# Two products by tiles, a pinned order of early casts, squares and copies, one pipeline for eight chunks

## The chip, the cores and the metric

The kernel runs on one core of one Trainium2 chip. The metric is the device time of one execution in microseconds (us); lower is better. A core has five engines that run independent instruction streams: TensorE (PE, matmuls; the load of its stationary operand is shown as PEld), VectorE (DVE), ScalarE (ACT), GpSimd (POOL), and a sync engine (SP) whose queue starts most of the transfers. Each stream is executed in the order in which it was written down; an instruction that waits holds up what stands behind it on its engine. Results of TensorE lie in eight banks of PSUM, all else in SBUF.

## What is computed

One layer on a sequence of 1024 tokens of width 1024, in float32: a feed-forward block, a mixer (a gated convolution on half of the channels, a gated delta rule with four heads on the other half), another feed-forward block, a norm. Cut to what matters:

```python
h = h + 0.5 * swiglu_ffn(rmsnorm(h, ffn1_norm), ffn1_w_in, ffn1_w_out)
u = rmsnorm(h, mix_norm) @ w_mix_in
cb, cc, ch, gq, gk, gv, gz, gb, ga = split(u)
y_conv = short_conv_mixer(cb, cc, ch, conv_short_w, conv_out_norm)      # 3 taps, norm over groups of 64
# q, k, v pass a causal convolution of 4 taps and silu; then, chunk by chunk,
# a triangular solve, products with a state that is carried on, norm, gate silu(z)
y_gdn = gated_deltanet_mixer(gq, gk, gv, gz, gb, ga, gdn_conv_w, ...)
h = h + concatenate([y_conv, y_gdn]) @ w_mix_out
h = h + 0.5 * swiglu_ffn(rmsnorm(h, ffn2_norm), ffn2_w_in, ffn2_w_out)
return rmsnorm(h, final_norm)
# swiglu_ffn(x): gate, up = split(x @ w_in);  (silu(gate) * up) @ w_out
```

## The kernel before

**Products.** Activations lie transposed, in tiles of 128 channels x 512 tokens; the tokens are two halves. Each float32 operand is split into a rounded high part (`hi`, `whi`, a cast on ScalarE) and a low part (`lo`, `wlo`, a subtraction on VectorE; `split`, lines 99 to 104), and one product of a tile is three matmuls of 128x512 (`mm3`, lines 190 to 194). Projections with two weight blocks and two token halves are done as 2x2 block products with seven multiplications instead of eight (`Pair`): products 1 and 2 take the first half of the tokens alone (`run_p1`, `run_p2`), 5 and 6 sums of halves with differences of weights (S1 with T1, nS2 with T2), 7 S3 with T3, 4 A22 with T4, 3 S4 with B22. T1 to T4 are made by GpSimd from raw weights in a ring of four buffers, then split; raw weights lie in a ring of eight, split ones in rings of seven. The first norm enters with `norm1` and `split1`; the second token half waits for its norm factor `rb`, which TensorE spreads over the partitions (L243), and then `sums` makes S1, nS2, S3, S4, A22 on VectorE and GpSimd (lines 293 to 320). `c22` at L389 is the first result of product 7.

**Order.** The program is written as lists of steps with a load, a preparation and a run (`task`, `run_tasks`); a scheduler then places the instructions on each engine by its own estimate of times. `tc.keep_in_program_order` pins an instruction behind those of its engine that were written before it. `later(n, f)` runs f after n further groups of three matmuls.

**Stages.** The first feed-forward block takes its first 100 us to start (`first_heads`, `by_tokens`: squares by tokens of the second half on ScalarE, L233; `begin2`: gains, L290). Then follow its body, its second product, the q, k, v projection (690 to 822 us) with the convolution of its first token half in `done`, and the delta rule: `build` makes the matrices of one chunk of 128 tokens, `solve` inverts, `finish` and `scan` carry the state through. The stage around 822 to 960 us builds chunks 0 to 3, then 4 and 5, with projections of z and of the short convolution (`rest`, through `pump`) between the steps at a rate `PACE`; `late` brings the convolution of the second token half. The scans of chunks 0 to 3 and of 4 to 7 are two pipelines (`inverse_and_scan`), the second beside the output projection `mix_out`. The second feed-forward block begins near 1250 us; the end of the kernel multiplies by the last factor, two quarters of the tokens after another, with one PSUM tile for both.

## Time and profile before

| | before |
|---|---|
| median of 3 executions | 1906.28 us (1905.80 to 1906.45) |
| the profiled execution, its span | 1906.43 us, 1904.4 us |
| TensorE busy in the span | 1816.6 us (95%) |
| VectorE, ScalarE, GpSimd busy | 1337.0 (70%), 747.3 (39%), 732.2 us (38%) |
| mean clock granted to TensorE | 0.981 of full speed |

A busy share is an average over stages with different limits, and TensorE's times overlap. So the views below go by stretches: which instruction waits there, and for which other.

### The profile page before, as it was taken

The numbers are of one execution on the slowest core, as the hardware profiler recorded it, in microseconds if no ns is written. First come the engines' busy times: TensorE is split into PE (matmuls) and PEld (weight loads), VectorE is DVE, ScalarE is ACT, GpSimd is POOL, SyncE is SP. The second block draws the span as 40 slices with busy tenths as digits, with TensorE's granted clock in tenths as the row PEclk, the third lists the DMA queues.
The fourth block names the chain that finished last, engine by engine and source line by source line (L and its number), as shares of the span: only waits on it lengthen the run. The fifth ranks groups of instructions, "written<-read, shape, count | busy, mean of one in ns | idle before, by whom it ended". The sixth has DMA issues, their size and how long they took to land.

```text
span 1904.4 us, 25000 instructions
## 1 busy us (share of the span) xinstructions
PE 1816.6 (95%) x8512; PEld 1483.8 (78%) x8512; DVE 1337.0 (70%) x1997; ACT 747.3 (39%) x1518; POOL 732.2 (38%) x514
## 2 busy tenths in 40 slices
PE   5799999999999998989899999999999999999997
PEld 4578888888888886777788888777788888888886
DVE  4876566657765888877868566787766666777666
ACT  5422232323434554367343333552222222344443
POOL 1464445445341434233321002035454455434243
PEclk9999999999999999999899989999999999999998
DMA  7143434345984543368744375422443434388642
GB/s 281 42 165 107 144 110 158 116 141 182 314 275 141 166 139 105 128 202 258 233 149 131 111 261 188 157 95 96 132 164 115 137 111 165 130 294 285 210 133 94
DMA packets 195663, 312.44 MB, mean 164 GB/s; under 512 B 27984, under 2 KB 50512, under 8 KB 195536
## 3 DMA queue, kind: packets, MB, share of 16 engines
q1 hardware_dynamic: 192080, 305.54, 48.4%
q10 hardware_dynamic: 3456, 5.31, 0.9%
q8 instruction: 67, 1.10, 0.2%
q14 instruction: 60, 0.49, 0.1%
HBM read 228.44 MB, written 82.33 MB: 163 GB/s over the span
## 4 chain that ended last, share of the span: by engine, by line
PE 44%; DVE 4%; issue 1%; DMA 1%; ACT 1%; POOL 1%; SPq 0%; POOLq 0%; DVEq 0%; ACTq 0%
PE ps_ps L191 10%; PE ps_ps L193 10%; PE ps_ps L192 10%; PE ps_mm L191 3%; PE ps_mm L193 3%; PE ps_mm L192 3%; DVE wlo L103 1%; PE ps_aux L879 1%; DVE lo L103 1%; PE ps_aux L921 0%; PE ps_aux L1147 0%; PE ps_mm L1199 0%; PE ps_aux L1146 0%; PE ps_mm L1185 0%; PE ps_aux L885 0%
## 5 line engine op out<-in xcount | busy, mean ns | idle before, releaser
L191 PE MATMUL ps_ps<-hi,whi 128*128 128x512 f32 x1400 | 551.2, 394 | 22.1 <-DVE c L389 12.3
L193 PE MATMUL ps_ps<-hi,wlo 128*128 128x512 f32 x1400 | 550.6, 394 | 12.6 <-DVE wlo L103 12.6
L192 PE MATMUL ps_ps<-lo,whi 128*128 128x512 f32 x1400 | 550.1, 393 | 4.8 <-DVE lo L103 4.7
L103 DVE TENSOR_TENSOR wlo<-T,whi 128x512 fp32r<-128x512 f32 x244 | 239.3, 994 | 145.3 <-ACT whi L102 144.0
L103 DVE TENSOR_TENSOR wlo<-raw,whi 128x512 fp32r<-128x512 f32 x280 | 261.6, 952 | 101.6 <-ACT whi L102 98.5
L191 PEld LDWEIGHTS ps_ps<-hi,whi 128*128 128x128 f32 x1400 | 265.6, 190 | 84.0 <-issue 10.2
L193 PEld LDWEIGHTS ps_ps<-hi,wlo 128*128 128x128 f32 x1400 | 265.9, 190 | 71.2 <-DVE wlo L103 15.6
L192 PEld LDWEIGHTS ps_ps<-lo,whi 128*128 128x128 f32 x1400 | 265.6, 190 | 62.2 <-DVE lo L103 7.2
L110 POOL TENSOR_TENSOR T<-raw 128x512 f32<-128x512 f32 x144 | 225.9, 1570 | 229.3 <-DMA raw<-w_out 87.5
L193 PE MATMUL ps_ps<-ghi,wlo 128*128 128x512 f32 x616 | 241.2, 392 | 0.8 <-DVE wlo L103 0.8
L191 PE MATMUL ps_ps<-ghi,whi 128*128 128x512 f32 x616 | 241.2, 392 | 0.0
L192 PE MATMUL ps_ps<-glo,whi 128*128 128x512 f32 x616 | 240.9, 391 | 0.0
L102 ACT CAST whi<-raw 128x512 fp32r<-128x512 f32 x280 | 169.3, 618 | 61.7 <-DMA raw<-w_out 17.2
L102 ACT CAST whi<-T 128x512 fp32r<-128x512 f32 x244 | 146.4, 617 | 78.4 <-POOL T L110 45.0
L191 PE MATMUL ps_mm<-hi,whi 128*128 128x512 f32 x384 | 160.3, 417 | 4.8 <-ACT whi L102 3.9
L103 DVE TENSOR_TENSOR glo<-raw,ghi 128x512 fp32r<-128x512 f32 x154 | 129.8, 844 | 46.7 <-ACT ghi L102 45.5
L193 PE MATMUL ps_mm<-hi,wlo 128*128 128x512 f32 x384 | 152.9, 399 | 0.8 <-DVE wlo L103 0.8
L192 PE MATMUL ps_mm<-lo,whi 128*128 128x512 f32 x384 | 152.9, 398 | 0.0
L193 PEld LDWEIGHTS ps_ps<-ghi,wlo 128*128 128x128 f32 x616 | 115.8, 188 | 27.6 <-DVE wlo L103 2.1
L192 PEld LDWEIGHTS ps_ps<-glo,whi 128*128 128x128 f32 x616 | 115.9, 188 | 25.5
L191 PEld LDWEIGHTS ps_ps<-ghi,whi 128*128 128x128 f32 x616 | 115.8, 188 | 25.3
L110 POOL TENSOR_TENSOR T<-raw,T 128x512 f32<-128x512 f32 x50 | 71.3, 1426 | 165.8 <-DMA raw<-w_in 135.2
(222 smaller groups left out, 2271.2 us busy)
## 6 DMA issues: line engine op xcount, KB each, us to landing
raw<-w_in SPq DMA_DIRECT2D x264, 256.0 KB, 4.5
raw<-w_out SPq DMA_DIRECT2D x154, 256.0 KB, 4.2
raw<-w_qkv SPq DMA_DIRECT2D x36, 256.0 KB, 3.3
f1S<-S SPq DMA_DIRECT2D x33, 256.0 KB, 4.9
raw<-f1A SPq DMA_DIRECT2D x33, 256.0 KB, 3.6
raw<-f1S SPq DMA_DIRECT2D x33, 256.0 KB, 3.5
f2S<-S SPq DMA_DIRECT2D x33, 256.0 KB, 4.9
raw<-f2A SPq DMA_DIRECT2D x33, 256.0 KB, 4.7
```

Source lines behind the costliest of these rows:

```text
L102: tc.keep_in_program_order(nc.scalar.copy(out=hi, in_=src))
L103: nc.vector.tensor_tensor(out=lo, in0=src, in1=hi.bitcast(F32), op=ALU.subtract)
L110: tc.keep_in_program_order(nc.gpsimd.tensor_tensor(out=out, in0=in0, in1=in1, op=op))
L191: nc.tensor.matmul(out=ps, lhsT=whi, rhs=xhi, start=start, stop=False, skip_group_check=True)
L192: nc.tensor.matmul(out=ps, lhsT=whi, rhs=xlo, start=False, stop=False, skip_group_check=True)
L193: nc.tensor.matmul(out=ps, lhsT=wlo, rhs=xhi, start=False, stop=stop, skip_group_check=True)
L879: nc.tensor.matmul(out=ps[:, sl], lhsT=lhs[:, sl], rhs=rhs[:, sl], start=start, stop=stop)
```

## The change

The squares by tokens, the gains of `begin2` and the copies of the first products of the first five pairs are pinned in the order written. Products 5 and 6 of the first two pairs of each block run by tiles: for each of four tiles k the product T1 with S1[k] and T2 with nS2[k] (`both`), with S1[k] split as soon as it exists. `sums(1)` and `sums(2)` become tasks at other places. The convolution of v for the first half of the tokens leaves `qkv_pair` and is done from a stored copy in `late_convs`; v's transfer into a chunk stands at a later step of `build`. The rate `PACE` falls, the reduce of `conv_norm` comes three groups later, all eight chunks go through one pipeline of scans, the split of the second block's first half runs inside the last output projection, and the last factor gets two PSUM tiles.

```diff
-PACE = (3.0, 2.6)
+PACE = (2.8, 2.2)
...
             for i, tile_ in enumerate(src):
-                nc.scalar.activation(out=tile_, in_=tile_, func=AF.Square, accum_out=tot[:, i:i + 1])
+                tc.keep_in_program_order(
+                    nc.scalar.activation(out=tile_, in_=tile_, func=AF.Square, accum_out=tot[:, i:i + 1]))
...
-            nc.scalar.activation(out=h2[k], in_=h2[k], func=AF.Copy, scale=self.gain(k))
+            tc.keep_in_program_order(
+                nc.scalar.activation(out=h2[k], in_=h2[k], func=AF.Copy, scale=self.gain(k)))
...
+                    b["S1"][k] = split(s1, slot)
                     b["nS2"][k] = split(s2, slot)
-                for k in range(KH):
-                    b["S1"][k] = split(h[1][k], slot)
...
-            nc.scalar.copy(out=self.p1[:, 3:HALF + 3], in_=self.x_ps)
+            ins = nc.scalar.copy(out=self.p1[:, 3:HALF + 3], in_=self.x_ps)
+            if self.pinned:
+                tc.keep_in_program_order(ins)
...
+        def both(self, k):
+
+            if k == 0:
+                self.z, self.y = psum(), psum()
+            ks = slice(k * P, (k + 1) * P)
+            for ps, t, s in ((self.z, "T1", "S1"), (self.y, "T2", "nS2")):
+                w = self.w[t]
+                mm3(ps, w[0][:, ks], w[1][:, ks], *self.x.b[s][k], k == 0, k == KH - 1)
+            if k == KH - 1:
+                self.w.pop("T1"), self.w.pop("T2")
+                self.u2 = temp4(F32, "u2")
+                nc.vector.tensor_tensor(out=self.u2[:, 3:HALF + 3], in0=self.y, in1=self.p1[:, 3:HALF + 3], op=ALU.add)
...
-            for n, two in enumerate(zip(*(p.body() for p in pairs[a:a + 2]))):
-                if a == 0 and n in (1, 2):
-                    task(None, lambda n=n: norm2.then(lambda: x.sums(n, norm2.rb)))
-                for t in two:
-                    task(*t)
+            products = list(zip(*(p.body() for p in pairs[a:a + 2])))
+            if a == 0:
+
+                for one, two in zip(*products[:2]):
+                    task(None, one[1], one[2])
+                    task(None, two[1])
+                for k in range(KH):
+                    task(lambda k=k: [p.both(k) for p in pairs[:2]])
+            for n, two in enumerate(products):
+                if a == 0 and n == 1:
+                    task(None, lambda: norm2.then(lambda: x.sums(1, norm2.rb)))
+                if a > 0 or n > 1:
+                    for t in two:
+                        task(*t)
+                if a == 0 and n == 2:
+                    task(None, lambda: norm2.then(lambda: x.sums(2, norm2.rb)))
...
+            for p in early:
+                p.pinned = True
...
+        v_dr = [dram.tile([P, HALF + 3], F32, name=f"v_dr{n}") for n in range(HEADS)]
...
-                    conv4(n + i, 0, t1, temp(F32, "cv"))
+                    if n < 2 * HEADS:
+                        conv4(n + i, 0, t1, temp(F32, "cv"))
+                    else:
+                        nc.sync.dma_start(out=v_dr[n + i - 2 * HEADS], in_=t1[:, 0:HALF + 3])
...
-            for g, dst in ((1, kT), (0, qT), (2, vT)):
+            for g, dst in ((1, kT), (0, qT)):
...
+            yield
             yield
...
+            nc.sync.dma_start(out=heads(vT), in_=qkv_dr[2][hf][:, :, ts])
             pq2 = flip(qT)
...
-            later(4, reduce)
+            later(7, reduce)
...
-            for n in (4, 5, 6, 7, 0, 1, 2, 3, 8, 9, 10, 11):
+            first = [(n, 0, v_dr[n - 8]) for n in (8, 9, 10, 11)]
+            for n, hf, src in first + [(n, 1, u_dr[n]) for n in (4, 5, 6, 7, 0, 1, 2, 3, 8, 9, 10, 11)]:
                 u = halo(F32, "u")
-                nc.sync.dma_start(out=u[:, 0:HALF + 3], in_=u_dr[n])
+                nc.sync.dma_start(out=u[:, 0:HALF + 3], in_=src)
                 yield
-                conv4(n, 1, u, mx.tile([P, HALF], F32, name="cv", tag="acc", bufs=3))
+                conv4(n, hf, u, mx.tile([P, HALF], F32, name="cv", tag="acc", bufs=3))
...
-                next(rest, None)
+                if next(rest, rest) is rest:
+                    tick()
...
         def inverse_and_scan(c):
+            if c == CPH:
+                for _ in side:
+                    pass
             yield from finish(c)
             yield from scan(c)
+            scanned.add(c)
...
-        drive(pipeline([build(c) for c in range(CPH)], 3), PACE[0], late, 1)
+        builds = pipeline([build(c) for c in range(CPH)], 3)
+        for _ in range(6):
+            next(builds)
+            pump(PACE[0])
+            next(late), next(late)
+        drive(builds, PACE[0], late, 1)
...
-        drive(pipeline([inverse_and_scan(c) for c in range(CPH)], 5), PACE[1], side, 1)
-        for _ in side:
-            pass
+        scans = pipeline([inverse_and_scan(c) for c in range(NCH)], 5)
+        while CPH - 1 not in scanned:
+            next(scans)
+            pump(PACE[1])
+            next(side, None)
...
-                task(lambda u=u: run(u, 1))
+                task(lambda u=u: run(u, 1), also and (lambda u=u: also(u)))
...
-        for n in range(4):
+        for n in range(6):
             tick()
             next(scans)
...
-        task(None, lambda: [x2.split1(d) for d in range(KT)])
-        mix_out(1, 1)
+        mix_out(1, 1, lambda u: [x2.split1(d) for d in (2 * u, 2 * u + 1)])
...
-        last[1].rb = psum()
...
+        rbs = [psum() for _ in range(2)]
         for i in range(2):
             for b in range(2 * i, 2 * i + 2):
-                nc.tensor.matmul(out=last[1].rb[:, b * P:(b + 1) * P], lhsT=rs[:, b:b + 1].broadcast_to([P, P]),
+                nc.tensor.matmul(out=rbs[i][:, b * P:(b + 1) * P], lhsT=rs[:, b:b + 1].broadcast_to([P, P]),
                                  rhs=ident, start=True, stop=True)
+            last[1].rb = rbs[i]
             scale_out(1, slice(2 * i * P, (2 * i + 2) * P))
```

The order of instructions on ScalarE at the start of the first block: `hi<-h` are the casts of the first half's tiles for product 2, `xtok` the squares by tokens, `p_...` the copies of first products. Before:

```order
L102 CAST whi<-raw 128x512 x2
L233 ACTIVATE xtok,tot<-xtok 128x512 x6
L351 COPY p_439<-ps_ps 128x512
L233 ACTIVATE xtok,tot<-xtok 128x512 x2
L102 CAST whi<-raw 128x512
L351 COPY p_441<-ps_ps 128x512
L351 COPY p_443<-ps_ps 128x512
L351 COPY p_445<-ps_ps 128x512
L290 ACTIVATE h<-h,vs 128x512 x2
L351 COPY p_466<-ps_ps 128x512
L102 CAST whi<-raw 128x512
L102 CAST hi<-h 128x512
```

and now:

```order
L102 CAST whi<-raw 128x512 x2
L102 CAST hi<-h 128x512 x4
L234 ACTIVATE xtok,tot<-xtok 128x512 x8
L102 CAST whi<-raw 128x512
L352 COPY p_443<-ps_ps 128x512
L352 COPY p_445<-ps_ps 128x512
L352 COPY p_447<-ps_ps 128x512
L352 COPY p_449<-ps_ps 128x512
L352 COPY p_470<-ps_ps 128x512
L102 CAST whi<-raw 128x512
```

Four casts stand ahead of all squares, and the squares ahead of all copies; before, the first of these casts was behind them.

VectorE at the start of the q, k, v projection: the last rows up to the first `c` of product 7 (`s` are the sums S4, `T_...` the weight differences, `u` the results of product 6). Before:

```order
L103 TENSOR_TENSOR lo<-h,hi 128x512 x4
L380 TENSOR_TENSOR u_6428<-ps_ps,p_6123 128x512
L103 TENSOR_TENSOR lo<-s_6297,hi 128x512
L103 TENSOR_TENSOR lo<-s_6305,hi 128x512
L103 TENSOR_TENSOR lo<-s_6313,hi 128x512
L103 TENSOR_TENSOR lo<-s_6321,hi 128x512
L103 TENSOR_TENSOR wlo<-T_6430,whi 128x512
L103 TENSOR_TENSOR wlo<-T_6436,whi 128x512
L103 TENSOR_TENSOR wlo<-T_6461,whi 128x512
L103 TENSOR_TENSOR wlo<-T_6486,whi 128x512
L103 TENSOR_TENSOR wlo<-raw,whi 128x512 x2
L389 TENSOR_TENSOR c_6508<-ps_ps,p_6089 128x512
```

and now:

```order
L103 TENSOR_TENSOR wlo<-T_6388,whi 128x512
L103 TENSOR_TENSOR wlo<-T_6406,whi 128x512
L103 TENSOR_TENSOR lo<-h,hi 128x512 x4
L103 TENSOR_TENSOR lo<-s_6341,hi 128x512
L378 TENSOR_TENSOR u_6462<-ps_ps,p_6093 128x512
L103 TENSOR_TENSOR lo<-s_6349,hi 128x512
L378 TENSOR_TENSOR u_6470<-ps_ps,p_6127 128x512
L103 TENSOR_TENSOR lo<-s_6357,hi 128x512
L103 TENSOR_TENSOR lo<-s_6365,hi 128x512
L103 TENSOR_TENSOR wlo<-T_6478,whi 128x512
L103 TENSOR_TENSOR wlo<-T_6490,whi 128x512
L405 TENSOR_TENSOR c_6508<-ps_ps,p_6093 128x512
```

The two `wlo<-raw` ahead of `c` are gone from there, and two differences T have moved ahead of the low parts `lo`.

The sync queue in the build stage (`qkv_dr20` is v after its convolution, `gd_...` the tiles of a chunk, loaded from q, k, v; `u` the inputs of the late convolution). Before:

```order
L937 DMA st_kg0_7346<-gd_7306 128x512
L937 DMA st_kd0_7349<-gd_7317 128x512
L937 DMA st_qg0_7347<-gd_7303 128x512
L944 DMA gd_7307<-qkv_dr10_292 128x4x128
L944 DMA gd_7304<-qkv_dr00_290 128x4x128
L937 DMA st_lt0_7351<-gd_7319 128x512
L790 DMA qkv_dr11_293<-cv_7464 128x512
L993 DMA diag_l0_7394<-dl_7481 128x4x32
L937 DMA st_at0_7350<-gd_7314 128x512
L944 DMA gd_7310<-qkv_dr20_294 128x4x128
```

and now:

```order
L820 DMA qkv_dr20_294<-cv_7470 128x512
L1265 DMA z_dr1_7240<-s_7548 128x512
L1312 DMA u_7551<-u_dr5_305 128x515
L970 DMA st_qg0_7327<-gd_7283 128x512
L977 DMA gd_7286<-qkv_dr10_292 128x4x128
L820 DMA qkv_dr20_294<-cv_7505 128x512
L1312 DMA u_7582<-u_dr6_306 128x515
L820 DMA qkv_dr11_293<-cv_7524 128x512
L1265 DMA z_dr0_7239<-s_7655 128x512
L1039 DMA gd_7289<-qkv_dr20_294 128x4x128
L1312 DMA u_7662<-u_dr7_307 128x515
```

Stores of v's convolution and loads of its inputs stand between a chunk's transfers now, and the load of v (`gd<-qkv_dr20`) behind the last of those stores.

## Rows read from the trace of the kernel before

**Rows 1.** Busy time by stretch, whole kernel; columns: stretch and its length, then busy time and instructions of PE, weight load, DVE, ACT, POOL, then the clock that TensorE was granted (1.00 is 2.4 GHz), the share of DMA engines busy and GB/s.

```profile
238.00:333.00 95.00, 95.00 (x421) 78.65 (x420) 62.58 (x70) 27.34 (x50) 49.28 (x32) 1.00 0.40 133
822.00:960.00 138.00, 124.44 (x602) 101.18 (x602) 107.53 (x240) 81.63 (x208) 53.24 (x44) 0.94 0.76 244
1092.00:1120.00 28.00, 25.30 (x194) 21.80 (x195) 12.34 (x28) 9.51 (x26) 3.27 (x2) 0.76 0.54 160
1250.00:1300.00 50.00, 43.27 (x178) 34.03 (x177) 46.01 (x56) 24.18 (x43) 24.75 (x15) 0.93 0.18 59
```

**Rows 2.** Timeline, TensorE between 38 and 46 us: start, length, line, operation, count, and in brackets the idle time ahead of it and what ended that.

```profile
38.03 0.96 PE L191 MATMUL ps_ps<-hi,whi 128*128 128x512 f32 x3 [1.86 <-ACT hi L102]
40.90 0.80 PE L192 MATMUL ps_ps<-lo,whi 128*128 128x512 f32 x1 [1.92 <-DVE lo L103]
41.50 0.63 PE L193 MATMUL ps_ps<-hi,wlo 128*128 128x512 f32 x1
...
45.76 0.62 PE L191 MATMUL ps_ps<-hi,whi 128*128 128x512 f32 x1
```

**Rows 3.** Timeline, ScalarE in the same stretch: a copy of a first product, which had waited for TensorE, and the first of the late casts.

```profile
31.45 0.58 ACT L351 COPY p<-ps_ps 128x512 f32<-128x512 f32 x1 [3.83 <-PE ps_ps L193]
...
37.33 0.65 ACT L102 CAST hi<-h 128x512 fp32r<-128x512 f32 x1
```

**Rows 4.** Timeline, VectorE (first four rows) and GpSimd (last two) in the first feed-forward block, from the first sum with the second norm factor to the first c of product 7.

```profile
52.12 0.69 DVE L300 TENSOR_TENSOR h<-h,ps_ps 128x512 f32<-128x512 f32 x1 [0.95 <-PE ps_ps L243]
...
57.65 1.19 DVE L103 TENSOR_TENSOR lo<-h,hi 128x512 fp32r<-128x512 f32 x1
...
63.37 0.68 DVE L103 TENSOR_TENSOR lo<-h,hi 128x512 fp32r<-128x512 f32 x1
...
87.82 0.68 DVE L389 TENSOR_TENSOR c<-ps_ps,p 128x512 f32<-128x512 f32 x1
...
56.61 3.38 POOL L110 TENSOR_TENSOR s<-h 128x512 f32<-128x512 f32 x2 [1.23 <-DVE h L301]
...
72.19 3.90 POOL L110 TENSOR_TENSOR T<-raw 128x512 f32<-128x512 f32 x2 [9.90 <-DVE wlo L103]
```

**Rows 5.** Waits of TensorE between 46 and 100 us: line that waited, what ended the wait, total, number, longest.

```profile
PE ps_ps L193 <- DVE wlo L103: 7.0, 2, 6.1
PE ps_ps L191 <- DVE c L389: 2.9, 1, 2.9
```

**Rows 6.** Timeline, VectorE at the start of the q, k, v projection, the same places.

```profile
693.28 1.27 DVE L300 TENSOR_TENSOR h<-h,ps_ps 128x512 f32<-128x512 f32 x2
...
736.31 0.68 DVE L389 TENSOR_TENSOR c<-ps_ps,p 128x512 f32<-128x512 f32 x1
```

**Rows 7.** Waits of TensorE at the start of that projection (690 to 745 us).

```profile
PE ps_ps L193 <- DVE wlo L103: 3.0, 2, 2.2
PE ps_ps L191 <- DVE c L389: 2.5, 1, 2.5
```

**Rows 8.** Start of the second feed-forward block: the waits of TensorE for low parts of weights (1255 to 1300 us), and the timeline row of TensorE behind its wait for c.

```profile
PE ps_ps L193 <- DVE wlo L103: 2.6, 2, 2.2
...
1297.06 0.47 PE L191 MATMUL ps_ps<-hi,whi 128*128 128x512 f32 x1 [2.94 <-DVE c L389]
```

**Rows 9.** Costliest groups of instructions between 790 and 825 us, shapes apart: the filter taps and the first scaling of the convolution there (busy time, mean of one).

```profile
L787 DVE SCALAR_TENSOR_TENSOR cv<-u,vs,cv 128x512 f32<-128x512 f32 x12 | 9.0, 749 | 1.1 <-ACT cv L785 0.9
...
L785 ACT ACTIVATE cv<-u,vs 128x512 f32<-128x512 f32 x4 | 2.9, 722 | 0.0
```

**Rows 10.** The longest wait of TensorE between 790 and 825 us.

```profile
PE ps_ps L191 <- DVE c L389: 1.9, 1, 1.9
```

**Rows 11.** Waits of TensorE in the build stage (822 to 960 us), the two longest.

```profile
PE ps_mm L1185 <- ACT sq L1180: 4.5, 1, 4.5
PE ps_aux L885 <- DMA gd<-qkv_dr: 3.1, 1, 3.1
```

**Rows 12.** Timeline of the sync queue in the build stage: a store of the convolution (L790), and behind it the load of one chunk's k and q (L944).

```profile
903.84 0.32 SPq L790 DMA_DIRECT2D qkv_dr<-cv  x1
904.25 1.23 SPq L944 DMA_DIRECT2D gd<-qkv_dr  x2
```

**Rows 13.** Waits of TensorE from 1200 to 1245 us, where the attention output is projected for the second half of the tokens.

```profile
PE ps_mm L191 <- ACT whi L102: 3.0, 1, 3.0
...
PE ps_mm L193 <- DVE wlo L103: 0.8, 1, 0.8
```

**Rows 14.** Timeline, VectorE in that stretch: low parts of the normalised first half (lo<-h) ahead of those of the projection's own operands (lo<-raw, wlo<-raw).

```profile
1206.35 1.89 DVE L103 TENSOR_TENSOR lo<-h,hi 128x512 fp32r<-128x512 f32 x3
...
1212.99 2.49 DVE L103 TENSOR_TENSOR lo<-raw,hi 128x512 fp32r<-128x512 f32 x4
```

**Rows 15.** Timeline, the end of the kernel, all engines.

```profile
1892.96 1.22 PE L1461 MATMUL ps_ps<-cs,last_rs 128*128 128x128 f32 x4 [0.18 <-POOL last_rs L1458]
...
1894.62 2.05 DVE L1430 SCALAR_TENSOR_TENSOR h<-h,vs,ps_ps 128x256 f32<-128x256 f32 x5 [1.65 <-ACT rbs L1424]
1894.67 2.09 POOL L1428 TENSOR_TENSOR h<-h,rbs 128x256 f32<-128x256 f32 x3 [0.92 <-ACT rbs L1424]
...
1896.82 1.19 PE L1461 MATMUL ps_ps<-cs,last_rs 128*128 128x128 f32 x4 [2.63 <-POOL h L1428]
...
1898.45 2.05 DVE L1430 SCALAR_TENSOR_TENSOR h<-h,vs,ps_ps 128x256 f32<-128x256 f32 x5 [1.78 <-ACT rbs L1424]
```

More of the change, by code (lines that the diff above doesn't have):

```diff
@@ L328, in __init__ @@
             self.x, self.srcs, self.first, self.done = x, srcs, first, done
-            self.r, self.t, self.w = {}, {}, {}
+            self.r, self.t, self.w, self.pinned = {}, {}, {}, False
         def get(self, *names):
@@ L1302, in pipeline @@
                         yield
+        scanned = set()
         def inverse_and_scan(c):
+            if c == CPH:
+                for _ in side:
+                    pass
             yield from finish(c)
             yield from scan(c)
+            scanned.add(c)
         def drive(main, n_main, side, n_side):
@@ L1343, in tile_hybrid, with mix_out @@
         norms2 = [Norm(h2[0], "mm"), Norm(h2[1])]
-        def mix_out(part, hf, bank="mm"):
+        def mix_out(part, hf, also=None):
+            bank = "mm"
             ys, w = [], {}
@@ L1377, in mix_out @@
                 task(lambda u=u: run(u, 0), lambda u=u: ready(u), lambda u=u: loads(u))
-                task(lambda u=u: run(u, 1))
+                task(lambda u=u: run(u, 1), also and (lambda u=u: also(u)))
         run_tasks()
-        scans = pipeline([inverse_and_scan(c) for c in range(CPH, NCH)], 5)
-        for n in range(4):
+        for n in range(6):
             tick()
@@ L1390, in tile_hybrid @@
         mix_out(0, 1)
-        left = [len(tasks)]
         def between():
```

## The prediction

> **What bounds the kernel now.** I read the views in this order: busy shares and slices on the page, busy time by stretch, TensorE's waits in each stretch, and the timelines around the longest waits. In the middle of a feed-forward block TensorE is never idle at full clock: 421 instructions fill 95.00 us [rows 1], so 0.226 us is the pace of one 128x512 product instruction. The same number of matmuls stands in the changed program, so time can only come from waits, from the clock that falls in them, and from the two ends. The waits sit where a stage begins. The build stage (822 to 960 us) is 138.00 long with 124.44 busy at a clock of 0.94, the chain of scans at the join 28.00 with 25.30 at 0.76, the start of the second block 50.00 with 43.27 at 0.93 [rows 1]. A mean clock of 0.94 with levels of 1.2 and 2.4 GHz says that 12% of the stretch ran at the lower level, 16.6 us, of which half, 8.3, is lost; with 13.6 idle the build stage gives at most 21.9. The join likewise: 13.4 us at the lower level, 6.7 lost, 2.7 idle, at most 9.4.
>
> **The change part by part.**
>
> *Early casts, squares and copies.* TensorE stops for 1.86 us on a cast (hi, ScalarE) and 1.92 on the low part (lo, VectorE), and the ten products from 41.50 to 45.76 then take 4.26 where ten at full pace take 2.26, 2.0 lost [rows 2]. The cast at 37.33 stands behind a first product's copy that had waited 3.83 for TensorE itself [rows 3]. In the new order four casts stand ahead of the eight squares and of all copies, so both stops go, and with them most of the half clock: 3.8 + 2.0 = 5.8. The squares come 4 casts later, 4 x 0.65 [rows 3] = 2.6 us, but no longer behind the copy, so the norm factor is not late: nothing for that if so, 2.6 if not. Taken: 6 with a little more half clock than the ten show; 3 to 7.
>
> *Products 5 and 6 by tiles, S1 split at once.* In the first block VectorE runs from the first sum with the second factor (52.12) to the first c of product 7 (87.82) nearly without pause [rows 4]: 35.7 us for 46 instructions, counted in the order, 0.776 each. TensorE waits in that stretch 7.0 for wlo and 2.9 for c [rows 5]. In the new order 41 instructions stand between the same two; three of the five that go are low parts of weights that now come later. 41 x 0.776 = 31.8, so c comes 3.9 earlier relative to the first sum. What waits for the postponed weights is late next: after c the program has one VectorE instruction per product or so and room for them. Gain here 3.9; 1 if they return as a wait behind c, 8 if VectorE drops to its short rows of 0.68 [rows 4] (41 x 0.68 = 27.9, 7.8 less). With the casts, 10 for the first block; 4 to 15.
>
> On the contention: one lo is 0.68 us long by itself and 1.19 beside a sum on GpSimd (3.38 for two) [rows 4]; so GpSimd costs VectorE about 0.5 us an instruction there, inside my 0.776. The Trainium skill (SBUF — State Buffer, Who interferes with whom) says more: a VectorE instruction with two inputs in SBUF and a GpSimd instruction that reads SBUF exclude each other for the whole length of the one that began. By that rule the reordering could buy nothing in these starts, which is rival B below; the row, 0.5 lost where the GpSimd instruction lasts 1.7, speaks against the full length.
>
> *The same at the two later starts.* In the projection the same two places are 693.28 and 736.31 apart by 43.0 us, 50 instructions, 0.861 each [rows 6]; 48 stand there now, so 41.3 and 1.7 gained if VectorE is the whole story. TensorE's waits there are 3.0 and 2.5 [rows 7]; all of both gone would be 5.5, with a little half clock 7. GpSimd's T waited 9.90 for a buffer in the first block [rows 4]; with product 5 and 6 eating T1 and T2 side by side these buffers come free together. I take the middle, 4.5; 1.5 to 7. The second block has 52 instructions, now 49, and waits 2.9 and 2.6 [rows 8]: 3 x 0.861 = 2.6 to 5.5 plus half clock (0.93 in 50.00 us [rows 1]: 7 us low, 3.5 lost); 4.5; 1.5 to 8.
>
> *v's convolution late.* Twelve taps of 0.749 us and four scalings of 0.722 [rows 9] leave the end of the projection, where TensorE's longest wait is 1.9 for c on VectorE [rows 10]: that wait goes, 2; 0 to 3. They come back in the build stage: 9.0 us on VectorE, which is busy 107.53 of 138.00 there, and ScalarE 81.63 of 138.00 [rows 1], with four stores and four loads more in the sync queue.
>
> *Build stage.* Two things push the other way. The reduce of conv_norm stands seven steps behind its square, not four: three steps of three products, 9 x 0.226 = 2.0 us off the 4.5 us wait [rows 11], and with it some of the low clock behind it. The other long wait, 3.1 for a chunk's k and q, came from the sync queue: its load at 904.25 was issued right behind a convolution's store at 903.84 [rows 11, 12]. v's load now stands behind v's stores, but only where it is needed, later than k's and q's. More tasks between the steps at the start (7 x 2.8 against 6 x 3.0) cover the rest. Gain 3; from -8 (v's work all on the path: 9.0) to 10 (half of the 21.9).
>
> *One pipeline of eight chunks.* At the join the fourth scan no longer runs alone; the fifth chunk's steps lie beside it. The output's flip still follows its scan directly, and the small products of two chains cannot fill the gap, so I keep half: 4.5 of the 9.4, less a little for the thinner cover elsewhere (2.2 against 2.6): 4; 0 to 7.
>
> *x2.split1 in pieces.* TensorE waits 3.0 and 0.8 on operands of the projection [rows 13], since low parts of the normalised half (1206.35) go first on VectorE, ahead of the projection's own (1212.99) [rows 14]. Two per step instead of eight ahead: 3.8, and the earlier end of the scans; 4; 2 to 5.
>
> *Last factor in two tiles.* The second pair of matmuls (1896.82) waits 2.63 for GpSimd's readers of the first half [rows 15]. In its own tile it follows the first pair (1892.96 + 1.22 = 1894.18, four more end near 1895.4), its copy is done by 1895.8, and VectorE takes the second half when it ends the first, 1894.62 + 2.05 = 1896.67 instead of 1898.45: 1.8; 1 to 2.6.
>
> *Sum.* 10 + 4.5 + 4.5 + 2 + 3 + 4 + 4 + 1.8 = 33.8. The profiled execution took 1906.43 us (span 1904.4), 0.15 above the median of three, 1906.28: 1906.4 - 33.8 = 1872.6, so 1872. The ends of the terms added are 12 and 57 or so; independent errors of that kind add to about 9.
>
> **The rivals.** *B: VectorE's chain sets the starts.* If the two projections of c move by nothing and only the cast (6), the tail (1.8), the split in pieces (4), the join (2) and the end of the projection (2) stay: 15.8 saved, 1890.6. For it: the chain from the first sum to c has no pause in the first block [rows 4]. Against it: fewer instructions stand in it now. Chance 0.18.
>
> *C: the starts close.* If every wait at the three starts goes (6 + 9.9, 7, 8) and the build stage gives 8: 30.9 + 8 + 2 + 4 + 4 + 1.8 = 50.7, 1855.7. For it: TensorE's waits name single operands, each of which comes earlier. Against it: VectorE's 0.776 per instruction. Chance 0.13.
>
> *D: the sync queue starves the chunks.* Each chunk's k, q, v loads stand in one in-order queue behind stores that wait for VectorE and ScalarE. Should each of the eight chunks stop TensorE as the one of 3.1 us did [rows 11], with about 2 of low clock behind it as after the casts [rows 2], that is 5 x 8 = 40 us, less the one there is, 35; against 30.8 of the other terms this is 1910.6. It decides from about seven such stops. For it: v's stores and their queue places. Against it: only one such stop in the present kernel. Chance 0.04.
>
> *E: the early casts do not free TensorE, nor the rest,* since the factor is late by the squares: then about 1903 to 1908. Chance 0.02.
>
> **How the numbers follow.** Forecast 0.63, B 0.18, C 0.13, D 0.04, E 0.02. The forecast's own errors reach from 1861 to 1884; the range takes in B's 1890.6 and reaches nearly to C's 1855.7, 1856 to 1891, which leaves about 2 in 10 out. Over 0.2% is 3.8 us, about what a measurement of this kernel can tell from no change: faster 0.94, within 0.02, slower 0.04.
>
> **What would show it.** Right: the eight squares of ScalarE behind the four casts, no stop of TensorE near 38 and no half clock behind it; the first c of product 7 in the first block near 78 instead of 87.8; waits for wlo and c at 690 to 745 and 1250 to 1300 below 4 together; the second pair of the last factor directly behind the first. Wrong: a norm factor that comes later; a wait for wlo of T3 or T4 as long as before; TensorE stops in the build stage on loads from v_dr or on v's stores; the join at a clock of 0.76 as before.

## The result, and the profile after

The changed kernel takes 1890.75 us in the median of 4 executions (1887.05 to 1893.83), the kernel before 1906.13 in 4 (1905.80 to 1906.45): a ratio of 0.9918 with an interval of 0.9896 to 0.9941, faster by 15.4 us. The forecast was 1872, so the sign was right and the size less than half of the 33.8 us forecast. The profiled execution is the fastest of the four, 1887.05 us with a span of 1885.3: it shows a gain of 19.4, and the other 4 or so of the median are, as far as later profiles of the same kernel show, a matter of the clock (experiment 1). TensorE is busy 1803.2 us of it instead of 1816.6.

To see where the gain arose I took, from the two traces, the time at which each kernel starts its n-th product instruction of 128x512 and subtracted. This lead is worked out from all rows of TensorE and stands in no view; between 830 and 1230 us the two programs run other small products between these, so only the values at both ends of that stretch are to be compared. At each time the first such product at or after it in the kernel before is taken.

```
time in the kernel before    45   88  100  690  745  790  822  960 1240 1350 1880
lead of the changed one     7.5 10.5  7.1  6.7  6.9  6.9  7.7  7.6 14.9 18.9 18.6
```

The terms of the sum beside it: first block 10 forecast, 6.7 found (7.1 at 100, 6.7 after it); start of the projection 4.5 and 0.2; end of the projection 2 and 0.8; build stage 3 and -0.1; pipeline of scans and split in pieces 4 + 4 and 7.3; start of the second block 4.5 and 4.0; end 1.8 and 0.5 (19.1 at the end of the span).

**Early casts.** TensorE between 30 and 46 us, the kernel before and then the changed one (columns as in [rows 1]): the stops are gone, and the clock is full.

```profile
30.00:46.00 16.00, 12.22 (x43) 9.29 (x42) 9.72 (x13) 11.11 (x21) 8.15 (x5) 0.79 0.45 161
30.00:46.00 16.00, 16.00 (x75) 13.12 (x74) 8.73 (x12) 12.66 (x25) 7.29 (x5) 1.00 0.56 198
```

**First block.** TensorE's waits between 46 and 100 us, which answer to [rows 5]:

```profile
PE ps_ps L191 <- DVE c L405: 3.0, 1, 3.0
PE ps_ps L191 <- DVE u L378: 2.2, 1, 2.2
PE ps_ps L192 <- DVE lo L103: 1.9, 4, 0.7
PE ps_ps L193 <- DVE wlo L103: 1.1, 1, 1.1
```

The waits on wlo are down from 7.0 to 1.1, the wait on c is as long as before, and one on u (the result of product 6) is new. VectorE's timeline, first sum with the second factor, first u, first c, against [rows 4]:

```profile
45.66 0.67 DVE L302 TENSOR_TENSOR h<-h,ps_ps 128x512 f32<-128x512 f32 x1
...
66.97 0.68 DVE L378 TENSOR_TENSOR u<-ps_ps,p 128x512 f32<-128x512 f32 x1
...
77.35 0.68 DVE L405 TENSOR_TENSOR c<-ps_ps,p 128x512 f32<-128x512 f32 x1
```

From 45.66 to 77.35 are 31.69 us for 41 instructions, 0.773 each; the forecast had 31.8. The first sum comes 6.5 us earlier, as the early casts promised, and c 10.5. But then TensorE's clock falls: in stretches behind the two longest stops (columns as in [rows 1])

```profile
78.00:88.00 10.00, 9.82 (x28) 7.09 (x29) 9.30 (x14) 1.14 (x2) 3.27 (x2) 0.66 0.01 2
723.00:735.00 12.00, 11.68 (x45) 9.57 (x46) 10.96 (x18) 2.59 (x6) 2.96 (x2) 0.86 0.01 1
```

the granted clock is 0.66 in the ten us behind the wait on c, 3.4 us lost: fourteen products take 6.7 us, at 0.43 us or more each instead of 0.23 (the clock there is 0.66 in the three later profiles of this kernel too). In the kernel before the low clock lay behind its long wait on wlo, and the like stop of 2.9 us on c, which ended at 88.6, was followed by full clock:

```profile
70.00:81.00 11.00, 8.08 (x25) 6.15 (x25) 11.00 (x18) 6.02 (x11) 3.97 (x3) 0.69 0.15 48
88.00:98.00 10.00, 9.36 (x41) 7.80 (x42) 8.60 (x14) 2.81 (x5) 3.41 (x3) 1.00 0.06 24
```

So the low clock did not go, it moved behind c, and that is the 3.4 us that the lead gives back between 88 and 100.

**Start of the projection.** TensorE's wait there, where [rows 7] had wlo with 3.0 and c with 2.5:

```profile
PE ps_ps L191 <- DVE u L378: 6.0, 1, 6.0
```

and VectorE and GpSimd:

```profile
686.58 1.27 DVE L302 TENSOR_TENSOR h<-h,ps_ps 128x512 f32<-128x512 f32 x2
...
715.17 1.16 DVE L103 TENSOR_TENSOR wlo<-T,whi 128x512 fp32r<-128x512 f32 x1 [1.83 <-ACT whi L102]
716.25 5.72 DVE L103 TENSOR_TENSOR lo<-h,hi 128x512 fp32r<-128x512 f32 x4
...
722.50 0.68 DVE L378 TENSOR_TENSOR u<-ps_ps,p 128x512 f32<-128x512 f32 x1
...
727.82 0.69 DVE L405 TENSOR_TENSOR c<-ps_ps,p 128x512 f32<-128x512 f32 x1 [1.04 <-PE ps_ps L193]
```

```profile
708.06 6.42 POOL L110 TENSOR_TENSOR T<-raw 128x512 f32<-128x512 f32 x1 [2.60 <-DVE wlo L103]
...
714.49 2.99 POOL L110 TENSOR_TENSOR T<-raw,T 128x512 f32<-128x512 f32 x2
```

c comes 41.2 us after the first sum with 48 instructions, beside the 41.3 of the forecast; 2.9 of them are pauses (1.83 and 1.04 above), the second one for product 7 itself. But TensorE may not go on with product 7 in the PSUM tile of product 6 before VectorE has read that into u, and u stands in VectorE's order behind four low parts of A22, which took 5.72 us: the first three lasted about 1.75 us instead of 0.68, each beside a difference on GpSimd. Before, product 5 in its own PSUM tile lay between product 6 and product 7 and hid that. One difference on GpSimd took 6.42 us at 708.06. VectorE worked beside it without a pause up to 713.3 and then stood for 1.83 us, since the cast that it waited for (whi) needs that difference.

**Build stage.** TensorE's waits (against [rows 11]), and the sync queue ahead of the longest (L1039 is v's load, L820 a store of the late convolution):

```profile
PE ps_aux L918 <- DMA gd<-qkv_dr: 7.8, 3, 4.6
PE ps_mm L1234 <- ACT rw L1231: 2.6, 2, 1.4
...
PE ps_mm L1220 <- ACT sq L1215: 1.4, 1, 1.4
```

```profile
843.83 0.32 SPq L820 DMA_DIRECT2D qkv_dr<-cv  x1
...
844.72 0.52 SPq L1039 DMA_DIRECT2D gd<-qkv_dr  x1
```

The reduce of conv_norm waits 1.4 instead of 4.5, but its second product 2.6, where before it waited 0.3; beside them come three stops on loads of a chunk, 7.8 us in all, 4.6 the longest. v's load was issued at 844.72, behind a store at 843.83 that waited for a silu of k's convolution, which it has nothing to do with.

**End.** The second half now follows the first, against [rows 15], and the rate of the transfers in forty slices of 0.4 us from 1870 to 1886:

```profile
1874.42 2.39 PE L1508 MATMUL ps_ps<-cs,last_rs 128*128 128x128 f32 x8
...
1876.06 4.00 DVE L1477 SCALAR_TENSOR_TENSOR h<-h,vs,ps_ps 128x256 f32<-128x256 f32 x10 [1.31 <-ACT rbs L1471]
...
1876.57 5.95 SPq L1479 DMA_DIRECT2D out_dram<-h  x10
```

```profile
GB/s 0 0 0 0 0 0 0 0 0 0 0 0 0 0 0 0 0 0 133 351 333 343 346 330 343 330 348 341 351 328 338 343 346 323 18 0 0 0 20 0
```

VectorE does its ten instructions without a pause, 1876.06 to 1880.06, and so ends 1.9 us earlier after the first of these products than before, as forecast. But the sixteen transfers then run at 323 to 351 GB/s from their first to their last byte, and they end the kernel: 2.1 MB at 340 GB/s are 6.2 us. In the kernel before the rate fell away for two such slices between the halves (1889 to 1905 us):

```profile
GB/s 0 0 0 0 0 0 0 0 0 0 0 0 0 0 0 0 0 172 346 336 336 351 338 336 341 69 8 318 338 346 338 333 348 341 254 0 0 0 0 0
```

Closing that hole is the gain: from the first product of the last sums to the last byte of the output it is 11.0 us instead of 11.7.

### The profile page after: what moved, and what is told of

It is laid out like the page before. It is cut to its first block, busy times and chain, and to the rows that moved or that the text cites. A ratio compares the mean times of both kernels' runs of the same rounds, so it can differ in the third digit from the quotient of the medians.

```text
span 1885.3 us, 25011 instructions
## 1 busy us (share of the span) xinstructions
PE 1803.2 (96%) x8512; PEld 1475.8 (78%) x8512; DVE 1333.0 (71%) x1997; ACT 747.9 (40%) x1518; POOL 740.6 (39%) x514
## 4 chain that ended last, share of the span: by engine, by line
PE 77%; DVE 12%; issue 3%; ACT 3%; DMA 2%; POOL 2%; SPq 0%; DVEq 0%; POOLq 0%; ACTq 0%
PE ps_ps L191 21%; PE ps_ps L193 21%; PE ps_ps L192 21%; PE ps_mm L191 3%; DVE wlo L103 3%; PE ps_mm L192 3%; PE ps_mm L193 3%; DVE lo L103 2%; PE ps_aux L912 1%; DVE cv L817 1%; DMA raw<-w_in 1%; DVE sv L1083 1%; DVE h L303 1%; PE ps_aux L918 1%; DVE xb L1087 1%
## 5 line engine op out<-in xcount | busy, mean ns | idle before, releaser
L110 POOL TENSOR_TENSOR T<-raw,T 128x512 f32<-128x512 f32 x50 | 77.8, 1556 | 156.7 <-DMA raw<-w_in 130.5
```

The lines of the kernel that those rows point to most:

```text
L110: tc.keep_in_program_order(nc.gpsimd.tensor_tensor(out=out, in0=in0, in1=in1, op=op))
```

## The experiments

All are compared with the kernel before on the same chip. That kernel has medians of 1904.2 to 1906.3 there; times of single kernels are compared with the changed one's on the same chip where it ran there, and places by leads over it, from one profile of each. u_later, no_tiles, v_early and two_pipes ran together on a chip on which the changed kernel did not; they stand against its medians on the other chips.

**1. The changed kernel again, three times (again, again2, again3).** No edit.

> The changed kernel once more, unaltered. Its four times so far lie between 1887.05 and 1893.83 us, where the kernel before stays within 0.7 us. Theory 1 (a race between transfers and the sync queue in the build stage): a profile near 1893 differs from the first one there, between 815 and 1000 us, by 4 to 6 us, and nowhere else. Theory 2 (a start of a stage that sometimes falls to the low clock): the difference sits at 46 to 100, 700 to 740 or 1250 to 1300 us, 2 to 4 us at each.

> The changed kernel a third time, on the chip of the three below, to compare them with. 1886 to 1894 by its nine times so far. Theory 1 (the same stops, with or without the low clock behind them, make the spread): its profile has the waits of the first two to 0.3 us each, and differs in the granted clock of single stretches.

> The changed kernel on the chip of the two below. All theories: 1885 to 1894, with the waits of its earlier profiles and one of the two levels of the clock at 975 to 1015 and at 1088 to 1135 us.

Medians 1889.89, 1890.50 and 1888.24 us; over all 20 executions of the changed kernel 1885.12 to 1893.83. Two stretches of the first profile of it and then of the second, which is 6 us longer (columns as in [rows 1]):

```profile
975.00:1015.00 40.00, 38.16 (x258) 31.97 (x257) 19.43 (x56) 19.12 (x65) 12.98 (x10) 1.00 0.57 181
1088.00:1135.00 47.00, 42.18 (x325) 36.58 (x324) 28.16 (x60) 19.89 (x56) 4.69 (x4) 0.96 0.77 244
```

```profile
975.00:1015.00 40.00, 38.15 (x238) 32.14 (x237) 16.68 (x47) 17.75 (x62) 13.66 (x11) 0.91 0.50 162
1088.00:1135.00 47.00, 42.09 (x307) 35.95 (x305) 25.56 (x54) 19.57 (x57) 5.29 (x4) 0.89 0.73 237
```

TensorE is busy to 0.1 us as long in both, with fewer instructions, since the granted clock is 0.91 instead of 1.00 and 0.89 instead of 0.96. The longest stops in the two stretches are the same to 0.1 us (1.5 in the first, 2.8 and 1.2 in the second). Behind like stops the clock falls in one execution and not, or for a shorter time, in another; by leads that is 3.0 and 2.8 us at these two places. In twelve profiles of the changed kernel and of its variants the second stretch has one of the two levels, 0.96 or 0.89. Theory 2 of the first expectation names the mechanism, but not the places; the transfers of theory 1 are not it.

**2. u ahead of A22's low parts (u_first, u_later).** In `all_pairs`, for all three starts, then for the two later ones alone:

```diff
-                if a == 0 and n == 2:
+                if a == 0 and n == 3:            # u_first
+                if a == 0 and n == (2 if x.g == V_N["ffn1"] else 3):   # u_later
                     task(None, lambda: norm2.then(lambda: x.sums(2, norm2.rb)))
```

> The changed kernel, with the split of A22 and S4 (sums(2)) written two tasks later, so that VectorE reads product 6 into u ahead of the low parts of A22. Theory 1 (the reordering put u late: TensorE may not go on with product 7 in the same PSUM tile before u is read, and u stands behind four low parts that take 5.7 us): TensorE's wait on u at the start of the q, k, v projection falls from 6.0 us to under 2, with the low clock behind it, and the kernel is 3 to 6 us faster than the changed one. Theory 2 (VectorE's chain up to c sets the start whatever stands where): the wait comes back on c or on a T, and the time stays within 1.5 us of the changed kernel.

> The changed kernel with u ahead of A22's low parts in the projection and the second feed-forward block only; the first block as in the changed kernel. Theory 1 (u's place matters where VectorE has the low parts of A22 still ahead of it; in the first block c is the limit): wait on u in the projection about 3 instead of 6 us, no low clock behind it, 4 us there and 0 to 1 in the second block: 1885 to 1886. Theory 2 (VectorE's chain decides at every start): within 1.5 us of the changed kernel.

u_first 1888.58 us (0.9910, 0.9894 to 0.9925), u_later 1884.98 (0.9894, 0.9876 to 0.9911). TensorE's wait on u in the projection with u_later:

```profile
PE ps_ps L191 <- DVE u L378: 3.1, 1, 3.1
```

It is halved, and the lead over the changed kernel goes from 0.7 at 690 to 3.5 at 737. That is theory 1 for the projection, though not its sizes: the wait is 3.1 in u_first too, not under 2, and behind it the clock is 0.91 from 720 to 737 us in u_later (1.00 in u_first, which gains 4.1 there). In the second block, where up to 1 us was expected, u_later loses 1.2 (3.6 at 1240, 2.4 at 1350). In the first block the same edit lengthens the wait on c, with u_first

```profile
PE ps_ps L191 <- DVE c L405: 6.2, 1, 6.2
```

and costs 2.0 (a lag behind the changed kernel of 2.9 at 88 us, of 0.9 at 45): there two differences and T4's low parts move ahead of c, and c is what TensorE waits for. That is theory 2. Each holds in its stage.

**3. GpSimd's differences (pool_less, u_pool, before_pool).** T3 and T4 of the first two pairs on VectorE, in the changed kernel, in u_later, and in the kernel before:

```diff
             self.t[n] = tt_tile(n)
-            pool_tt(self.t[n], p, q, op)
+            if self.on_vector and n in ("T3", "T4"):
+                nc.vector.tensor_tensor(out=self.t[n], in0=p, in1=q, op=op)
+            else:
+                pool_tt(self.t[n], p, q, op)
```

> The changed kernel with T3 and T4 of the first two pairs of each block made by VectorE instead of GpSimd: four more instructions of 0.6 us on VectorE, four fewer of 1.6 on GpSimd. Theory 1 (a GpSimd instruction costs VectorE about 0.5 us): the first c of product 7 moves by less than 1 us, and the time by less than 1.5. Theory 2 (the two exclude each other for the whole length, 1.6 us each): c comes 3 to 4 us earlier at each of the three starts, 4 to 10 us faster in all.

> The changed kernel with both edits: u ahead of A22's low parts in the projection and the second block, and T3 and T4 of the first two pairs on VectorE. Theory 1 (two causes, one in the order and one in the length of VectorE's instructions): the lead over the changed kernel at 745 us is 7 to 8 (3.4 and 5.2 alone), the wait on u gone, about 1881. Theory 2 (one cause: u comes late, by either): 5 to 6 at 745, no faster than with GpSimd's part alone.

> The kernel before with T3 and T4 of the first two pairs on VectorE. Theory 1 (GpSimd's differences cost VectorE about 1 us each, and T3 also waited for a buffer): c comes 2 to 3 us earlier in the first block and 4 in the projection, the wait for wlo of 6.1 us in the first block shrinks, 4 to 8 us faster than the kernel before. Theory 2 (only together with the tiles, which put T1 and T2 first): within 2 us of the kernel before.

pool_less 1881.04 us (0.9883, 0.9863 to 0.9903). First sum and first c on VectorE in the first block, and what is left of TensorE's waits in the projection:

```profile
47.09 0.67 DVE L302 TENSOR_TENSOR h<-h,ps_ps 128x512 f32<-128x512 f32 x1
...
76.34 0.68 DVE L408 TENSOR_TENSOR c<-ps_ps,p 128x512 f32<-128x512 f32 x1
```

```profile
PE ps_ps L193 <- DVE wlo L103: 1.5, 2, 1.1
PE ps_ps L191 <- ACT hi L102: 1.1, 1, 1.1
```

29.25 us for 45 instructions, 0.650 each, where the changed kernel has 31.69 for 41. Five GpSimd instructions fewer stand in it (5 instead of 10); four more of 0.6 on VectorE are 2.4, so the five cost VectorE 2.44 + 2.4 = 4.8 us, 1.0 each. Neither theory's number: more than 0.5, less than the 1.6 that one lasts (the next part says why). In the projection the lead grows by 4.3 (1.1 at 690, 5.4 at 737), and the wait on u is 0.4 instead of 6.0.

u_pool takes 1878.21 us (0.9856, 0.9831 to 0.9882), the fastest kernel here. The clock in the same two stretches as above for the changed kernel, and the wait on u:

```profile
78.00:88.00 10.00, 9.08 (x39) 6.89 (x38) 9.30 (x13) 2.23 (x4) 3.28 (x2) 1.00 0.10 35
723.00:735.00 12.00, 12.00 (x54) 9.68 (x54) 11.38 (x19) 4.17 (x8) 0.10 (x1) 1.00 0.23 89
```

```profile
PE ps_ps L191 <- DVE u L381: 2.7, 1, 2.7
```

The clock is 1.00 in both; it is low ahead of them instead, 0.72 from 66 to 78 us, where this kernel waits 4.6 for a cast (hi) and hardly for c, and 0.83 from 713 to 723. At 745 us the lead over the changed kernel is 6.6, between the two theories, but 2.7 of it were there at 100. From 100 to 745 u_pool gains 3.9, pool_less 4.0 and u_later 3.4: the two edits don't add, which speaks for one cause, u that comes late, by place or by GpSimd (theory 2 of u_pool). Why the wait on u is 2.7 with both edits and 0.4 with GpSimd's alone stays open. At 790 us u_pool is 0.6 ahead of pool_less; of the other 9.8 between their two profiles 4.4 are the clock at the places of experiment 1 and 2.2 lie near the end (1840 to 1860), so the 2.8 us between their medians are not shown to be the order's doing. before_pool takes 1898.75 us (0.9967, 0.9956 to 0.9979). Its wait in the first block:

```profile
PE ps_ps L193 <- DVE wlo L103: 7.2, 2, 6.1
```

This is as long as before, and the projection gains 0.7; 3.7 us come at the second block. There I had expected the first block, so theory 1 is right in the sum and wrong in the place.

**4. Without the tiles (no_tiles).** Products 5 and 6 whole, S1 split after all sums:

```diff
-                for k in range(KH):
-                    task(lambda k=k: [p.both(k) for p in pairs[:2]])
...
+            for n, two in enumerate(zip(*(p.body() for p in pairs[a:a + 2]))):
+                if a == 0 and n in (1, 2):
+                    task(None, lambda n=n: norm2.then(lambda: x.sums(n, norm2.rb)))
```

> The changed kernel with products 5 and 6 of the first pairs whole again, S1 split after all sums, sums(1) and sums(2) at their old places. Theory 1 (the early casts gain 7 us, of which VectorE's chain gives half back unless the tiles shorten it; in the projection the tiles only swap the waits for wlo and c for one for u): the lead at 100 us falls by 3.5, nothing at 745, about 4 at 1300, so 7 to 8 us slower than the changed kernel, near 1897. Theory 2 (the terms of my forecast: 4 + 4.5 + 4.5): 13 us slower, near 1903, with 4.5 of it in the projection.

1896.57 us (0.9954, 0.9938 to 0.9971), 6 to 8 slower than the changed kernel. By leads it loses 2.4 up to 100 us, nothing in the projection, 5.8 at the second block (and in this one profile 3.8 near 1870, where the tiles have no part). The waits in the projection are those of [rows 7] to 0.1 us:

```profile
PE ps_ps L193 <- DVE wlo L103: 2.9, 2, 2.3
PE ps_ps L191 <- DVE c L406: 2.5, 1, 2.5
```

Theory 1: there the tiles only swap these two for the one on u.

**5. Three parts alone (headtail).** The pins, the split in pieces and the two tiles of the last factor in the kernel before; edits as in the change.

> The kernel before with three parts of the change alone: the pinned order of squares, gains and copies, the split in pieces inside the last output projection, and the last factor in two tiles. By my terms 6 + 4 + 1.8 = 11.8 us, so 1894.3. Rival for the end: the output transfers set it, not VectorE; then it gives 0.5 instead of 1.8 and the kernel is at 1895.6. Rival for the split in pieces: the earlier end of the scans was most of it, and it gives 1 here.

1898.35 us (0.9962, 0.9948 to 0.9976), 6.5 faster and not 11.8. The lead is 7.5 us at 45, 6.5 at 88 and 3.7 at 100. The casts give more than forecast. VectorE's chain is 35.7 us long as before and begins 6.5 earlier, so c comes 6.5 earlier and costs only 1.0 of the lead; the other 2.8 go behind the wait on c, where the clock is now low:

```profile
PE ps_ps L193 <- DVE wlo L103: 7.5, 2, 7.0
PE ps_ps L191 <- DVE c L393: 2.9, 1, 2.9
```

```profile
81.00:91.00 10.00, 8.87 (x27) 7.13 (x28) 6.77 (x11) 1.63 (x3) 3.12 (x2) 0.66 0.02 5
```

The wait on wlo has grown from 7.0 to 7.5 and the one on c stayed. The split in pieces brings 3.4 (5.3 at 1214, 8.7 at 1220), of which 1.6 go again behind c in the second block (8.3 at 1294, 6.7 at 1302); the end brings 1.2 from the last sums to the last byte.

**6. Without the pins (no_pins).** `tc.keep_in_program_order` taken off squares, gains and copies, as before.

> The changed kernel without the pinned order of squares, gains and copies. Theory 1 (VectorE's chain gives half of the early casts' gain back): 3 to 4 us slower than the changed kernel. Theory 2 (with the tiles the chain is short enough, so the casts' 7 us count in full): 6 to 8 us slower.

1893.32 us (0.9932, 0.9920 to 0.9944) beside 1890.50 of the changed kernel on that chip, 2.8 slower. The lead over the changed kernel is -6.8 at 45 us and -4.8 at 100. So with the tiles the casts keep 4.8 of 6.8, without them 3.7 of 7.5. By the medians theory 1 is nearer; that VectorE's chain takes the gain back, which it names as the cause, is not what experiment 5 shows.

**7. Stores on ScalarE's queue (act_store).**

```diff
-            nc.sync.dma_start(out=qkv_dr[n // HEADS][hf][:, n % HEADS, :], in_=acc)
+            (nc.sync if n < 4 and hf == 0 or 4 <= n < 8 and hf == 0 else nc.scalar).dma_start(out=qkv_dr[n // HEADS]...
```

> The changed kernel, with the stores of the late convolutions issued from ScalarE's queue instead of the sync queue. Theory 1 (the loads of v and k, q for a chunk stand in the sync queue behind stores that wait for ScalarE's silu): TensorE's stops on loads of a chunk in the build stage (4.6, 2.1 and 1.1 us) go, with some low clock, 4 to 8 us faster than the changed kernel. Theory 2 (the data come late anyway, since VectorE and ScalarE carry v's convolution): the stops come back with another releaser, 0 to 2 us either way; up to 3 slower if the issues hold up ScalarE.

1904.07 us (0.9991, 0.9983 to 1.0000), 14 slower than the changed kernel. Its waits from 820 to 1010 us:

```profile
PE ps_aux L954 <- DMA xc<-diag_x: 6.8, 1, 6.8
PE ps_mm L191 <- ACT whi L102: 5.6, 1, 5.6
PE ps_aux L918 <- DMA gd<-qkv_dr: 2.9, 2, 2.1
```

The stops on a chunk's loads fall from 7.8 to 2.9, but ScalarE comes late with casts (5.6), and a load of the solve stops TensorE for 6.8; by leads 12 of the loss come between 960 and 1092 us, with that stop. The fall does not prove theory 1: TensorE stood for the cast directly ahead of where it had waited for v's load, and v's load was issued at 848.4 instead of 844.7. Theory 2 is right on the direction, and its 3 us far too small.

**8. v's convolution early (v_early, and best with u_later).** `done` calls conv4 for v again, `late_convs` and the first six steps as before.

> The changed kernel with v's convolution of the first token half back in the projection and without its extra steps; v's load keeps its late place. Theory 1 (v's load stands in the sync queue behind stores that wait for the late convolution): the stops on that load at 848 and 887 us go, the projection's end loses 1, net 3 to 6 us faster than the changed kernel. Theory 2 (the stops hide behind other late work of the build stage; the VectorE time is what counts): the end of the projection is 1 to 2 later and the build stage as long, 0 to 2 us slower.

> The changed kernel with u ahead of A22's low parts in the projection and the second block, and with v's convolution back in the projection: the two edits that were faster by themselves. Theory 1 (they are in different stages and add): 1880 to 1882. Theory 2 (v's place gave nothing but luck with the clock): 1884 to 1886, as with the first alone.

v_early 1885.05 us (0.9892, 0.9874 to 0.9910); best 1886.11 (0.9886, 0.9865 to 0.9907; 1877.87 to 1891.25). Waits on a chunk's loads in the build stage of v_early:

```profile
PE ps_aux L914 <- DMA gd<-qkv_dr: 7.1, 5, 2.1
```

Five stops, 7.1 us, in place of three of 7.8: v's late convolution by itself did not make them. By leads v_early goes from -0.3 at 790 to 0.7 at 1092, and best is not faster than u_later, theory 2 of best. So v's place is worth about 1 us, if anything; the 5 us between the medians of v_early and of the changed kernel are not shown to be its doing.

**9. Two pipelines (two_pipes).** `inverse_and_scan` in two pipelines of four, four steps ahead of the output projection, `later(4, reduce)`, as before.

> The changed kernel with two pipelines of scans as before, four scan steps ahead of the output projection and the reduce of conv_norm after four steps. Theory 1 (one pipeline lets the last four scans end earlier beside the output projection): the lead between 1092 and 1240 us falls by about 7, 6 to 9 us slower. Theory 2 (the join costs as much as the overlap gains, with a thinner cover before it): within 2 us of the changed kernel, since the leads lost between 960 and 1144 come back.

1894.09 us (0.9940, 0.9920 to 0.9960), 4 slower than the changed kernel by the medians, 8.5 by the leads at 1240. At 1092 and 1144 it is 3 ahead of the changed one, from 1144 to 1240 it falls back by 12. The wait for the projection's operands, gone in the changed kernel, is there again in spite of the pieces:

```profile
PE ps_mm L191 <- ACT whi L102: 4.1, 2, 3.2
```

So one pipeline costs some 3 us up to the join, and gains beside the output projection, where the scans end earlier. The edit on the reduce is in it too and was not run apart, nor was the lower `PACE` in any run.

## Why the prediction was wrong

In the profiled execution 14.7 of the 33.8 us are missing: 4.3 at the start of the projection, 3.3 in the first block, 3.1 in the build stage, 1.3 at the end and 1.2 at the end of the projection are the large pieces. The median lies some 4 us lower still, by the clock.

*Early casts:* right in the mechanism, 7.5 instead of 6 at 45 us. That the gain would stay was not: alone it keeps 3.7, with the tiles 4.8, and what goes alone goes in the main to a low clock behind the wait on c (5, 6).

*Products by tiles, first block:* the chain came out as sized, 41 x 0.776 = 31.8 against 31.69, in part by chance: 2.0 of the 35.7 us behind the 0.776 were pauses (0.733 without them), and the new chain has none. The step that failed is the next one, that TensorE gains what c gains. c came 10.5 us earlier, and 3.4 of it went into fourteen products at the low clock behind the unchanged wait of 3.0. I had counted the low clock that goes, and none that could come.

*The start of the projection:* again c came as worked out, 41.2 us after the first sum, and again in part by chance: 2.9 of it are pauses, one of them for TensorE itself, where the 43.0 us behind the 0.861 had 2.0. The step "TensorE's waits there are 3.0 and 2.5", of which I took the middle, 4.5 with some half clock, failed: they went, and the wait on u with 6.0 took their place, because product 7 follows on product 6 in one PSUM tile and VectorE's read of it lay behind four low parts. The order of VectorE that stands ahead of the prediction shows u there; I counted the instructions up to c and did not ask which of them TensorE would wait for. Experiments 2 and 3 show this cause from two sides.

*GpSimd beside VectorE:* my 0.5 us was the price of a sum; the differences T cost about 1.0 (3). I took a loss below the 1.6 or 1.7 us of a GpSimd instruction for a sign against full exclusion, and that reading was wrong. One pair in the projection:

```profile
717.43 1.72 POOL L110 TENSOR_TENSOR T<-raw 128x512 f32<-128x512 f32 x1
717.95 1.75 DVE L103 TENSOR_TENSOR lo<-h,hi 128x512 fp32r<-128x512 f32 x1
```

lo ends at 719.70, 0.55 us behind the difference (719.15). In the changed kernel's trace all 260 instructions of VectorE with two SBUF operands that began while a GpSimd instruction of this kind ran, and lasted over 0.8 us, end 0.55 or 0.56 us behind it, and GpSimd's own takes 1.29 (median of 41) where no such instruction of VectorE stands beside it: the 1.6 to 1.7 hold some 0.4 of its own waiting. So the rows agree with the rule of the Trainium skill (SBUF — State Buffer, Who interferes with whom) that the two exclude each other for a whole instruction. What VectorE loses is the part that is left of GpSimd's when its own is due, 0.5 beside that sum, 1.07 in this lo. Rival B, which I hung on that rule, gave 1890.6 and so almost the measured time, but not by its mechanism: it has c move by nothing, and the chain up to c became 4.0, 1.8 and 4.5 us shorter at the three starts.

*The second block:* 4.5 forecast, 4.0 found, as c came 4.5 us earlier. The waits did not go as the prediction's sign wanted; with the 1.2 for wlo in the projection they are 5.9 together, not below 4 (1235 to 1285 us):

```profile
PE ps_ps L193 <- DVE wlo L103: 3.2, 1, 3.2
PE ps_ps L191 <- DVE c L405: 1.5, 2, 1.1
```

*v's convolution late and the build stage:* 2 + 3 forecast, 0.7 found. The reduce's wait shrank by 3.1, more than the 2.0 of the forecast, but 2.3 came back at its second product. That a chunk's stops on loads would not grow was wrong, 7.8 instead of 3.1. The mechanism of rival D did appear, at three chunks and not at seven. That v's late convolution by itself is at fault is refuted by v_early, which has 7.1 us of such stops without it; what makes the chunks' loads late stays open.

*Pipeline and pieces:* 8 forecast, 7.3 found; the place was wrong for the first, not the join but the output projection (9).

*The last factor in two tiles:* 1.8 for VectorE was right, but the term took VectorE's end for the kernel's end; the output transfers are the bound from 1877.4 on, 0.5 to 1.2 found.

*The range:* the low ends of the terms add to 2, not to 12, with the -8 of the build stage; the range was not built on that figure.

## What to carry to other kernels

An order that brings an operand earlier is worth what the next wait leaves: list, for the instruction that waits now, every operand and every reader of the tile that it overwrites, and find the last of them in the new order, not only the one that was last in the old. Where two accumulations that lay one after the other are run side by side, the read of the first loses its cover.

A stop of TensorE costs its length and the products at the low clock behind it; a change that shortens one stop and leaves another can keep the second's clock low. And an end that is made shorter for the engines must be held against the time of the transfers.

## What was not expected of the hardware

Behind equal stops the granted clock fell in one execution and not in another of the same program: 1.00, 0.96 or 0.91 from 975 to 1015 us, 0.96 or 0.89 from 1088 to 1135, up to 3 us at each. The changed kernel spreads over 9 us in 20 executions where the kernel before stayed within 0.7 us on the first chip; on other chips that one spread too, by 6 to 11 us.

VectorE's time per instruction from the first sum to c, pauses of up to 2 us in the first block and 3.9 in the projection included, is nearly the same in every kernel with the differences on GpSimd: 0.773 to 0.776 in the first block for 41 or 46 instructions (0.821 for 43 in u_first, where two more GpSimd instructions lie in it), 0.859 to 0.881 in the projection. It falls to 0.650 and 0.743 when five and four of GpSimd's instructions leave the stretch. One GpSimd difference took 6.42 us: it ended only when VectorE, which had run nine instructions without a pause beside it, stood still.
